# Row sums moved behind the eighth up product, and layer 1's key and value products split into a pass for the latents and a pass for the context

## The chip, the cores and the metric

The kernel runs on one core of one Trainium2 chip. The metric is device time in microseconds (us), the median of the runs. A core has a matmul engine (PE; its weight loads are shown as PEld), a vector engine (DVE), a scalar engine (ACT), GpSimd (POOL) and a sync engine (SP) on whose queue all the loads of this kernel are issued. Each engine works through its own instructions in a fixed order; semaphores tie the engines together.

## The reference

Two layers of a diffusion transformer run over 256 latent tokens and 256 context tokens (512 columns here, latents first), with a model width of 1024. What matters is this part of each layer:

```
mod = silu(c) @ W_mod + b_mod                  # six vectors of 1024, for latents (c) and for context (c_ctx)
h   = rms_norm(x) * (1 + mod_scale) + mod_shift
k, v of four token mixers come from h @ W_in   # first used here: keys and values of the neighbourhood mixer
... attention, gates, output projection, x = x + mod_gate * y
h   = rms_norm(x) * (1 + mod_scale2) + mod_shift2
u   = h @ W_up                                 # 2 x 2816 columns: 22 pairs of 128-column tiles g, v
u   = depthwise conv of 3 taps along the tokens
x   = x + mod_gate2 * ((silu(g) * v) @ W_down)
```

`W_mod` gives 48 tiles of 128 outputs per layer. In layer 1 the context is needed for keys and values only.

## The kernel before, in words

Every matrix product is made of three matmuls per 128-row slice: high parts times high parts, and the two mixed terms with a low part (`mm3`, lines L278, L279, L280). So the weights are split on arrival: `wload` loads a raw tile of 128x1024 (L264, SP's queue), ACT casts its high part `wh` (L272) and DVE subtracts to give the low part `wl` (L257). There are four buffers each for raw, high and low weight tiles. The accumulators `acc` have three buffers of 512 columns in PSUM, `av` one.

The normed activations are made chunk by chunk, eight chunks of 128 channels, by `modulate`: DVE makes `t`, ACT makes the high part `hh` (L423), DVE makes the low part `hl`. The factor of the norm comes by `rstd`: PE sums over the partitions into `tp` (L402), DVE makes `v` (L404), POOL makes `r`, PE spreads it into `sc` (L408), from which DVE reads it for each `t`. That is done for the latents and for the context apart.

`mods` makes modulation vectors by row sums: it loads a 128x1024 tile of `W_mod` (L339, SP's queue, its own pool of four buffers in the stretch that matters here) and DVE multiplies it by the conditioning vector and sums along the row (L349, output `junk`, in the trace one long instruction and the short read of its accumulator). Inside layer 0's FFN there are 56 tiles with 80 row sums: 24 tiles with two sums each, 32 tiles with one. They are the gate of layer 0's FFN and vectors of layer 1.

The FFN of layer 0 begins with four up tiles whose weights are held while they run over the latents' 256 columns and then over the context's 256 columns: eight products of 24 matmuls of 256 columns. Then 40 up products of 512 columns follow (24 matmuls each), the first eight products of the down projection after the first 20 up tiles, and the rest of it at the end. The first three half-width products run together, chunk by chunk, as the modulated chunks come in. After each up product `conv` evacuates it: ACT makes `u`, and DVE adds two taps (`u<-acc`, L254). The product's `acc` is free after the second tap. In the code the eight half-width products come first, then the other products are written interleaved with `mods`. A scheduler moves instructions within each engine against that order, and in the kernel before it put many row sums ahead: 32 of the 80 ran during the output projection and the eight half-width products.

Layer 1 begins with `nakv`, the keys and values of the first mixer: four token tiles (0 and 1 latents, 2 and 3 context) over eight chunks, four accumulators open at once, all four advanced chunk by chunk. The products `naq` (256 wide) follow.

Of the kernel before, what the change touches and what calls it, by code (L numbers as in the profile page):

```python
# [3 lines left out]

# [9 lines left out]
ALU = mybir.AluOpType  # L14
# [5 lines left out]
P = 128  # L20
KD = D // P
# [210 lines left out]
def backbone(ctx: ExitStack, tc, wb, xT, cc, cb, sm, rg, bias, cst, out):  # L232
# [15 lines left out]
    V, A, G = nc.vector, nc.scalar, nc.gpsimd  # L248

    def spool(es, name, bufs, **k):  # L250
        return es.enter_context(tc.tile_pool(name=name, bufs=bufs, reuse_waits="tile", **k))

    def stt(out, in0, scalar, in1, op0, op1):
        V.scalar_tensor_tensor(out=out, in0=in0, scalar=scalar, in1=in1, op0=op0, op1=op1)  # L254

    def tt(e, out, a, b, op):
        e.tensor_tensor(out=out, in0=a, in1=b, op=op)  # L257

    def lo_of(lo, full, hi):
        tt(V, lo, full, hi.bitcast(F32), ALU.subtract)  # L260

    def wraw_load(l, key, n=1024):
        r = wraw.tile([P, 1024], F32, name="raw")
        nc.sync.dma_start(out=r[:, :n], in_=wb[l, KIDX[key], :, :n])  # L264
        return r

    def wload(l, key, k, n):

        w = k * n
        r = wraw_load(l, key, w)  # L270
        h = whi.tile([P, 1024], F32R, name="wh")
        A.copy(h[:, :w], r[:, :w])  # L272
        lo = wlo.tile([P, 1024], F32R, name="wl")
        lo_of(lo[:, :w], r[:, :w], h[:, :w])
        return tuple(z[:, :w].rearrange("p (k n) -> p k n", k=k) for z in (h, lo))

    def mm3(ps, a, b, first, last):
        mm(ps, lhsT=a[0], rhs=b[0], start=first, stop=False)  # L278
        mm(ps, lhsT=a[0], rhs=b[1], start=False, stop=False)  # L279
        mm(ps, lhsT=a[1], rhs=b[0], start=False, stop=last)  # L280

    def drive(*gens):

        live = [[g, n, 0] for g, n in gens]
        while live:
            e = min(live, key=lambda e: (e[2] + 0.5) / e[1])
            try:
                next(e[0])
                e[2] += 1
            except StopIteration:  # L290
                live.remove(e)
# [17 lines left out]
    cact = const.tile([P, 2, D], F32, name="cact")  # L309
    junk = const.tile([P, D], mybir.dt.bfloat16, name="junk")  # L310
    hh = hp.tile([P, KD, T], F32R, name="hh")
    hl = hp.tile([P, KD, T], F32R, name="hl")
# [3 lines left out]
    def small(l):  # L316
        smts[l] = lay.tile([P, NSM], F32, name="smt")
        nc.sync.dma_start(out=smts[l], in_=sm[l])
        Ms[l] = lay.tile([P, 48, 2], F32, name="M")
# [6 lines left out]
    plan = [(l, m, c) for l, m in [(0, 2), (0, 4), (0, 3), (0, 5), (1, 1), (1, 0), (1, 2), (1, 4), (1, 3), (1, 5)]  # L326
            for c in range(KD)]

    def mods(n, raws, ahead=0):


        todo = [plan.pop(0) for _ in range(n)]
        got = []

        def load():
            l, m, c = todo[len(got)]
            r = raws.tile([P, 1024], F32, name="raw")
            g = [g for g in range(3) if m in MOD_GROUPS[g]][0]
            nc.sync.dma_start(out=r, in_=wb[l, KIDX["mod", g, c, MOD_GROUPS[g].index(m)]])  # L339
            got.append(r)  # L340

        for i, (l, m, c) in enumerate(todo):
            while len(got) < min(i + 1 + ahead, n):
                load()
            r, M = got[i], Ms[l]
            ns = 1 if l == L - 1 and m > 1 else 2
            for st_ in range(ns):
                o = M[:, 8 * m + c, st_:st_ + 1]
                V.scalar_tensor_tensor(out=junk, in0=r, scalar=1.0, in1=cact[:, st_], op0=ALU.mult,  # L349
                                       op1=ALU.mult, accum_out=o)  # L350
            if c == KD - 1:
                b0 = SM["bmod"][0] + 8 * m
                bm = smts[l][:, b0:b0 + 8].unsqueeze(2).to_broadcast([P, 8, ns])
                tt(V, M[:, 8 * m:8 * m + 8, :ns], M[:, 8 * m:8 * m + 8, :ns], bm, ALU.add)
            yield

    def some(gen, n):

        for _ in range(n):
            next(gen)  # L360
            yield
# [34 lines left out]
    def rstd(accs, part):  # L396

        a, b, _ = part
        nt = (b - a) // P
        tp = tp_p.tile([P, T], F32, name="tp")  # L400
        for t in range(nt):
            mm(tp[:, t:t + 1], lhsT=accs[a][:, t * P:(t + 1) * P], rhs=ones[:, 0:1], start=True, stop=True)  # L402
        v = tiny.tile([P, 16], F32, name="v")
        V.tensor_scalar(out=v[:, :nt], in0=tp[:, :nt], scalar1=1.0 / D, scalar2=EPS, op0=ALU.mult, op1=ALU.add)  # L404
        r = pow_mhalf(v[:, :nt], nt)
        bc = sc_p.tile([P, T], F32, name="sc")
        for t in range(nt):
            mm(bc[:, t * P:(t + 1) * P], lhsT=r[:, t:t + 1].to_broadcast([P, P]), rhs=ident, start=True, stop=True)  # L408
        return bc
# [7 lines left out]
    def modulate(xt, bc, s1, M, msh, c, part):  # L417

        a, b_, s = part
        hs = tmp.tile([P, T], F32, name="t")[:, :b_ - a]  # L420
        b = M[:, 8 * msh + c, s:s + 1]
        stt(hs, xt[:, c, a:b_], s1[:, c, s:s + 1], bc[:, :b_ - a], ALU.mult, ALU.mult)
        A.activation(out=hh[:, c, a:b_], in_=hs, func=AF.Identity, bias=b)  # L423
        stt(hl[:, c, a:b_], hs, b, hh[:, c, a:b_].bitcast(F32), ALU.add, ALU.subtract)
# [55 lines left out]
    FULL = [(0, 256, 0), (256, 512, 1)]  # L480
    for l in range(L):
# [6 lines left out]
        if l == 0:  # L488
# [4 lines left out]
            xt = x0p.tile([P, KD, T], F32, name="x0")  # L493
# [12 lines left out]
        smt, M = smts[l], Ms[l]  # L506
        vec = lambda n, j=0, p=P: smt[:p, SM[n][0] + j:SM[n][0] + j + 1]
        gam1 = smt[:, SM["n1"][0]:SM["n1"][0] + 8]
        s1 = lay.tile([P, 8, 2], F32, name="s1")
        if l:  # L510
            mod_scale(M, gam1, 1, s1)
        else:
            mods_chunk(0)
            bcs = [rstd(accs, p_) for p_ in FULL]
# [401 lines left out]
        A2 = [0, 1]  # L916

        kv = [(acc_p if t < 3 else av_p).tile([P, 512], F32, name="acc" if t < 3 else "av") for t in range(4)]
        w = None
        for c in range(KD):  # L920
            if l == 0:
                if c:
                    mods_chunk(c)
                V.tensor_scalar(out=s1[:, c], in0=M[:, 8 + c], scalar1=1.0, scalar2=gam1[:, c:c + 1],
                                op0=ALU.add, op1=ALU.mult)
            for bc, p_ in zip(bcs, FULL):
                modulate(xt, bc, s1, M, 0, c, p_)
            if c % 2 == 0:
                w = wload(l, ("nakv", c // 2), 2, 512)
            for t in range(4):  # L930
                mm3(kv[t], tuple(z[:, c, t * P:(t + 1) * P] for z in (hh, hl)), tuple(z[:, c % 2] for z in w),
                    c == 0, c == KD - 1)

        rt = lay.tile([P, 2, 2, 2, RW], F32, name="rt", bufs=1)
        rgt = tmp.tile([P, 4, RW], F32, name="t")
# [18 lines left out]
        for t in range(4):  # L954
            p3 = kv[t].rearrange("p (a n) -> p a n", a=1)
            use_v("na")(t, 1, p3[:, :, 256:])
            later.extend([f, 0] for f in use_nk(t, 1, p3[:, :, :256]))
        first = chain(win_block(l, "naq", qh, use_qk(qT, "na", 4, 64, *q64, None, e=V)), flush())
        drive((first, 1))
        early = lambda n: [(mods(n, wraw), n)] if l == 0 else []  # L960
        newV("df"); newkq("df")
        PAIR = [(0, 1), (2, 3)]
# [26 lines left out]
        if l == 0:  # L989
            xp = ctx.enter_context(tc.tile_pool(name="xt", bufs=1, reuse_waits="tile"))  # L990
            xt = xp.tile([P, KD, T], F32, name="xt")
# [56 lines left out]
        s1 = lay.tile([P, 8, 2], F32, name="s1")  # L1048
# [7 lines left out]
        acts = {}  # L1056

        us = {}

        def up_ps(ff, w_, a, b):  # L1060
            ps = acc_p.tile([P, T], F32, name="acc")
            for kt in range(KD):
                mm3(ps[:, a:b], tuple(z[:, kt] for z in w_), (hh[:, kt, a:b], hl[:, kt, a:b]), kt == 0, kt == KD - 1)
            return ps

        def conv(ff, ps, a, b):

            cw = smt[:, SM["conv"][0] + 4 * ff:SM["conv"][0] + 4 * ff + 4]
            if ff not in us:
                us[ff] = up_.tile([P, T], F32, name="u%d" % (ff // NF))  # L1070
            u = us[ff]
            A.activation(out=u[:, a:b], in_=ps[:, a:b], func=AF.Identity, scale=cw[:, 1:2], bias=cw[:, 3:4])
            u3 = u[:, a:b].rearrange("p (s t) -> p s t", t=256)
            p3 = ps[:, a:b].rearrange("p (s t) -> p s t", t=256)
            stt(u3[:, :, 1:256], p3[:, :, 0:255], cw[:, 0:1], u3[:, :, 1:256], ALU.mult, ALU.add)
            stt(u3[:, :, 0:255], p3[:, :, 1:256], cw[:, 2:3], u3[:, :, 0:255], ALU.mult, ALU.add)

        def up_act(f):
            g, v = us.pop(f), us.pop(NF + f)
# [57 lines left out]
        if not last:  # L1137
            small(l + 1)
            accs = {}
            body = ffn(accs)  # L1140
            drive((some(body, 8), 8))
            mrp = spool(fes, "mr", 4)
            drive((body, 70), (mods(56, mrp, 2), 59))
        else:
            drive((ffn(None), 68))
        fes.close()
        if not last:
            bcs = accs["bc"]
# [22 lines left out]
```

## Time and profile before

| | |
|---|---|
| median of 3 runs | 1481.22 us (1481.22 to 1482.71) |
| profiled execution | 1481.19 us |
| its span, first to last instruction | 1479.4 us |
| PE busy | 1428.8 us, 97% of the span |
| DVE, ACT, POOL busy | 71%, 45%, 14% |
| mean granted clock of PE | 0.989 of full speed |

The shares are means over the whole span. In the stretches at the start of layer 0's FFN (about 565 to 609 us) and at the start of layer 1 (947 to 978 us) PE has gaps, and there it also ran at less than full clock.

### The profile page before, as it was taken

The numbers are of one execution on the slowest core, as the hardware profiler recorded it, in microseconds if no ns is written. First come the engines' busy times: TensorE is split into PE (matmuls) and PEld (weight loads), VectorE is DVE, ScalarE is ACT, GpSimd is POOL, SyncE is SP. The second block draws the span as 40 slices with busy tenths as digits, with TensorE's granted clock in tenths as the row PEclk, the third lists the DMA queues.
The fourth block names the chain that finished last, engine by engine and source line by source line (L and its number), as shares of the span: only waits on it lengthen the run. The fifth ranks groups of instructions, "written<-read, shape, count | busy, mean of one in ns | idle before, by whom it ended". The sixth has DMA issues, their size and how long they took to land.

```text
span 1479.4 us, 22328 instructions
## 1 busy us (share of the span) xinstructions
PE 1428.8 (97%) x8526; PEld 1197.5 (81%) x8526; DVE 1054.5 (71%) x1911; ACT 667.5 (45%) x1197; POOL 204.3 (14%) x191
## 2 busy tenths in 40 slices
PE   6999999999999997999999999899999999899999
PEld 3787777776777887888888888798788889799999
DVE  5688676658776589999856553668777575787884
ACT  5445544444333333444134432356646544564662
POOL 0343001213111200000000000034122331000000
PEclk9999999999999998999999999999999999999999
DMA  9532122214234364568822322333232344455553
GB/s 377 189 103 77 45 88 68 83 53 133 86 114 165 135 218 152 193 221 272 282 94 92 99 93 79 107 101 121 72 104 93 115 140 132 132 182 184 180 179 113
DMA packets 57931, 202.19 MB, mean 137 GB/s; under 512 B 6561, under 2 KB 8097, under 8 KB 57185
## 3 DMA queue, kind: packets, MB, share of 16 engines
q1 hardware_dynamic: 57824, 200.77, 40.2%
q8 instruction: 67, 1.10, 0.3%
q14 instruction: 40, 0.32, 0.1%
HBM read 199.69 MB, written 1.05 MB: 136 GB/s over the span
## 4 chain that ended last, share of the span: by engine, by line
PE 88%; DVE 6%; issue 3%; ACT 2%; DMA 1%; POOL 0%; SPq 0%; POOLq 0%; DVEq 0%; ACTq 0%
PE acc L278 24%; PE acc L280 24%; PE acc L279 24%; PE av L834 3%; PE sc L753 3%; PE tp L826 2%; DVE junk L349 2%; PE sc L768 2%; PE sc L767 1%; DVE wl L257 1%; ACT wh L272 1%; DVE t L254 1%; DMA raw<-in_wb_dram 1%; DMA mraw<-in_wb_dram 1%; PE acc L729 1%
## 5 line engine op out<-in xcount | busy, mean ns | idle before, releaser
L272 ACT CAST wh<-raw 128x1024 fp32r<-128x1024 f32 (+1 forms) x272 | 279.8, 1029 | 438.2 <-PE acc L279 336.6
L257 DVE TENSOR_TENSOR wl<-raw,wh 128x1024 fp32r<-128x1024 f32 (+1 forms) x272 | 331.4, 1218 | 158.7 <-ACT wh L272 156.3
L278 PE MATMUL acc<-hh,wh 128*128 128x256 f32 (+1 forms) x1248 | 424.7, 342 | 15.8 <-DVE u L254 8.7
L279 PE MATMUL acc<-hl,wh 128*128 128x256 f32 (+1 forms) x1248 | 419.4, 337 | 0.8 <-DVE hl L254 0.8
L280 PE MATMUL acc<-hh,wl 128*128 128x256 f32 (+1 forms) x1248 | 420.1, 337 | 0.0
L278 PEld LDWEIGHTS acc<-hh,wh 128*128 128x128 f32 x1248 | 239.8, 193 | 44.5 <-issue 12.9
L279 PEld LDWEIGHTS acc<-hl,wh 128*128 128x128 f32 x1248 | 240.6, 193 | 26.6 <-issue 3.3
L280 PEld LDWEIGHTS acc<-hh,wl 128*128 128x128 f32 x1248 | 240.5, 193 | 26.5 <-issue 4.3
L257 POOL TENSOR_TENSOR r<-v,mhalf 128x4 f32<-128x4 f32 (+3 forms) x59 | 81.6, 1387 | 736.5 <-DVE v L404 461.8
L349 DVE SCALAR_TENSOR_TENSOR junk<-raw,cact 128x1024 bf16<-128x1024 f32 x128 | 156.8, 1225 | 21.7 <-DMA raw<-in_wb_dram 21.1
L278 PE MATMUL acc<-wh,hh 128*128 128x256 f32 (+3 forms) x496 | 148.8, 300 | 4.2 <-ACT hh L423 4.2
L279 PE MATMUL acc<-wl,hh 128*128 128x256 f32 (+3 forms) x496 | 147.5, 297 | 0.0
L280 PE MATMUL acc<-wh,hl 128*128 128x256 f32 (+3 forms) x496 | 145.1, 298 | 0.1
L279 PE MATMUL acc<-al,wh 128*128 128x256 f32 (+1 forms) x370 | 121.5, 328 | 0.0
L278 PE MATMUL acc<-ah,wh 128*128 128x256 f32 (+1 forms) x370 | 121.5, 328 | 0.0
L280 PE MATMUL acc<-ah,wl 128*128 128x256 f32 (+1 forms) x370 | 121.4, 328 | 0.0
L254 DVE SCALAR_TENSOR_TENSOR u<-acc,smt,u 128x255 f32<-128x255 f32 (+1 forms) x184 | 108.4, 593 | 1.5
L278 PEld LDWEIGHTS acc<-wh,hh 128*128 128x128 f32 x496 | 94.9, 191 | 14.1 <-ACT hh L423 7.1
L776 ACT ACTIVATE p<-sc,nm 128x512 f32<-128x512 f32 (+1 forms) x120 | 74.1, 618 | 66.0 <-DVE nm L773 37.9
L280 PEld LDWEIGHTS acc<-wh,hl 128*128 128x128 f32 x496 | 94.5, 191 | 9.4 <-issue 5.5
L279 PEld LDWEIGHTS acc<-wl,hh 128*128 128x128 f32 x496 | 95.0, 191 | 6.8 <-issue 4.6
L773 DVE TENSOR_REDUCE nm<-sc 128x1 f32<-128x512 f32 (+1 forms) x120 | 71.1, 597 | 35.4 <-PE sc L768 24.8
(165 smaller groups left out, 2067.7 us busy)
## 6 DMA issues: line engine op xcount, KB each, us to landing
raw<-in_wb_dram SPq DMA_DIRECT2D x328, 512.0 KB, 3.4
mraw<-in_wb_dram SPq DMA_DIRECT2D x16, 512.0 KB, 10.2
raw<-in_wb_dram SPq DMA_DIRECT2D x20, 384.0 KB, 2.9
x<-in_xT_dram SPq DMA_DIRECT2D x2, 1024.0 KB, 6.3
bt<-in_bias_dram SPq DMA_DIRECT2D x8, 256.0 KB, 3.2
xt<-in_xT_dram SPq DMA_DIRECT2D x2, 1024.0 KB, 7.1
raw<-in_wb_dram SPq DMA_DIRECT2D x4, 320.0 KB, 2.8
cact<-in_cb_dram SPq DMA_DIRECT2D x1, 1024.0 KB, 11.4
```

Of the source, the lines that this page charges most:

```text
L254: V.scalar_tensor_tensor(out=out, in0=in0, scalar=scalar, in1=in1, op0=op0, op1=op1)
L257: e.tensor_tensor(out=out, in0=a, in1=b, op=op)
L272: A.copy(h[:, :w], r[:, :w])
L278: mm(ps, lhsT=a[0], rhs=b[0], start=first, stop=False)
L279: mm(ps, lhsT=a[0], rhs=b[1], start=False, stop=False)
L280: mm(ps, lhsT=a[1], rhs=b[0], start=False, stop=last)
L349: V.scalar_tensor_tensor(out=junk, in0=r, scalar=1.0, in1=cact[:, st_], op0=ALU.mult, op1=ALU.mult, accum_out=o)
L753: mm(sps[:, :n], lhsT=q[o:o + d, c:c + P], rhs=k[o:o + d, T - n:], start=True, stop=True)
L768: mm(sps[:, :n], lhsT=q[r1, 4 + i, c:c + P], rhs=kk[r1], start=False, stop=True)
L773: V.tensor_reduce(out=nm, in_=sps[:, :n], op=ALU.max, axis=AX.X, negate=True)
L776: A.activation(out=p[:, :n], in_=sps[:, :n], func=AF.Exp, bias=nm, accum_out=s)
L834: mm(av[64 * j:64 * j + 64], lhsT=V_[:, 4 - nk + i, vcol(hd):vcol(hd) + 64], rhs=PTs[j][:, i], start=i == 0, stop=i == nk - 1, tile_positi ...
```

## The change

The first part: the second tap of each `conv` is remembered in a list `behind`, and the `mods` call inside the FFN gets the last one that the eight half-width products left, the second tap of the eighth. Every row sum of the 56 tiles is given an ordering edge behind it. The loads of those tiles are given no such edge.

The second part: in layer 1 only, `nakv` first modulates the latents and makes the products of token tiles 0 and 1 for all eight chunks, keeping the four weight tiles; then it modulates the context and makes the products of tiles 2 and 3 for all eight chunks.

```
-    def mods(n, raws, ahead=0):
+    def mods(n, raws, ahead=0, behind=None):
...
-                V.scalar_tensor_tensor(out=junk, in0=r, scalar=1.0, in1=cact[:, st_], op0=ALU.mult,
-                                       op1=ALU.mult, accum_out=o)
+                with tc.issue_after(behind) if behind is not None else nullcontext():
+                    V.scalar_tensor_tensor(out=junk, in0=r, scalar=1.0, in1=cact[:, st_], op0=ALU.mult,
+                                           op1=ALU.mult, accum_out=o)
...
-        w = None
+        w = []
+
+        def kv_mm(c, t):
+            mm3(kv[t], tuple(z[:, c, t * P:(t + 1) * P] for z in (hh, hl)), tuple(z[:, c % 2] for z in w[c // 2]),
+                c == 0, c == KD - 1)
...
             for bc, p_ in zip(bcs, FULL):
-                modulate(xt, bc, s1, M, 0, c, p_)
+                if l == 0 or p_[2] == 0:
+                    modulate(xt, bc, s1, M, 0, c, p_)
             if c % 2 == 0:
-                w = wload(l, ("nakv", c // 2), 2, 512)
-            for t in range(4):
-                mm3(kv[t], tuple(z[:, c, t * P:(t + 1) * P] for z in (hh, hl)), tuple(z[:, c % 2] for z in w),
-                    c == 0, c == KD - 1)
+                w.append(wload(l, ("nakv", c // 2), 2, 512))
+            for t in range(4) if l == 0 else range(2):
+                kv_mm(c, t)
+        if l:
+            for c in range(KD):
+                modulate(xt, bcs[1], s1, M, 0, c, FULL[1])
+                for t in range(2, 4):
+                    kv_mm(c, t)
...
-            stt(u3[:, :, 0:255], p3[:, :, 1:256], cw[:, 2:3], u3[:, :, 0:255], ALU.mult, ALU.add)
+            tap = stt(u3[:, :, 0:255], p3[:, :, 1:256], cw[:, 2:3], u3[:, :, 0:255], ALU.mult, ALU.add)
+            behind.append(tap.ins)
...
-            drive((body, 70), (mods(56, mrp, 2), 59))
+            with_order = mods(56, mrp, 2, behind[-1])
+            drive((body, 70), (with_order, 59))
```

The numbers of instructions on every engine stay the same. The orders change as follows (lines of the changed kernel are one higher from L349 on).

On DVE, at the start of layer 0's FFN, the kernel before has this (a number at the end is a count of like instructions in a row):

```order
668 L349 SCALAR_TENSOR_TENSOR junk,M<-raw,cact 128x1024
669 L257 TENSOR_TENSOR wl<-raw,wh 128x1024
670 L254 SCALAR_TENSOR_TENSOR t<-xt,s_5389,sc 128x256 x2
671 L257 TENSOR_TENSOR ss<-ss,t 128x256
672 L349 SCALAR_TENSOR_TENSOR junk,M<-raw,cact 128x1024
673 L254 SCALAR_TENSOR_TENSOR hl<-t,M,hh 128x256
674 L254 SCALAR_TENSOR_TENSOR t<-xt,s_5389,sc 128x256
675 L254 SCALAR_TENSOR_TENSOR hl<-t,M,hh 128x256
676 L349 SCALAR_TENSOR_TENSOR junk,M<-raw,cact 128x1024
```

At the same place the changed kernel has this:

```order
652 L257 TENSOR_TENSOR wl<-raw,wh 128x1024
653 L254 SCALAR_TENSOR_TENSOR t<-xt,s_5389,sc 128x256 x2
654 L257 TENSOR_TENSOR ss<-ss,t 128x256
655 L254 SCALAR_TENSOR_TENSOR hl<-t,M,hh 128x256
656 L254 SCALAR_TENSOR_TENSOR t<-xt,s_5389,sc 128x256
657 L254 SCALAR_TENSOR_TENSOR hl<-t,M,hh 128x256
```

The row sums between the modulates are gone from here; the order of the rest is nearly the same.

On DVE, where the eighth half-width product (`u_5601`) has been evacuated, the changed kernel begins with the row sums, and from there on carries two of them, seldom one or three, in each of the next 38 products:

```order
696 L257 TENSOR_TENSOR wl<-raw,wh 128x1024
697 L254 SCALAR_TENSOR_TENSOR u_5601<-acc,smt,u_5601 128x255 x2
698 L350 SCALAR_TENSOR_TENSOR junk,M<-raw,cact 128x1024
699 L257 TENSOR_TENSOR u_5572<-u_5572,u_5601 128x512
700 L350 SCALAR_TENSOR_TENSOR junk,M<-raw,cact 128x1024
701 L257 TENSOR_TENSOR wl<-raw,wh 128x1024
702 L350 SCALAR_TENSOR_TENSOR junk,M<-raw,cact 128x1024
703 L257 TENSOR_TENSOR al<-u_5572,ah 128x512
704 L254 SCALAR_TENSOR_TENSOR u_5763<-acc,smt,u_5763 128x2x255
705 L350 SCALAR_TENSOR_TENSOR junk,M<-raw,cact 128x1024
```

So all 80 sums stand here and behind, where the kernel before had 48. On SP's queue the first four tiles of `W_mod` are issued where they were; behind them the changed kernel has twelve weight tiles in a row, and only then the fifth tile of `W_mod`, after which the two kinds alternate.

On PE, at the start of layer 1, the kernel before has the latents' `sc` products first, then the context's `tp`, and the context's `sc` after the first two products of chunk 0:

```order
4071 L408 MATMUL sc<-C,r 128x128 x2
4072 L402 MATMUL tp<-C,ss 128x1 x2
4073 L278 MATMUL acc<-wh,hh 128x512
4074 L279 MATMUL acc<-wl,hh 128x512
4075 L278 MATMUL acc<-wh,hh 128x512
4076 L279 MATMUL acc<-wl,hh 128x512
4077 L280 MATMUL acc<-wh,hl 128x512 x2
4078 L408 MATMUL sc<-C,r 128x128 x2
```

The changed kernel has the context's `tp` inside chunk 0, goes on with the latents' chunks 1, 2 and 3 from row 4079 on, and has the context's `sc` only in chunk 3, at row 4093:

```order
4072 L409 MATMUL sc<-C,r 128x128 x2
4073 L278 MATMUL acc<-wh,hh 128x512
4074 L279 MATMUL acc<-wl,hh 128x512
4075 L278 MATMUL acc<-wh,hh 128x512
4076 L279 MATMUL acc<-wl,hh 128x512
4077 L403 MATMUL tp<-C,ss 128x1 x2
4078 L280 MATMUL acc<-wh,hl 128x512 x2
4079 L278 MATMUL acc<-wh,hh 128x512
```

Nothing on PE stands between the latents' `sc` and their first product any more. DVE's order there begins as before with a `wl` and then has two latents' `t`, the context's last `ss`, and latents' `hl` and `t` in turn.

## Rows read from the trace of the kernel before

**Rows 1.** Waits of PE, 560 to 660: us in total, times, longest

```profile
PE acc L278 <- DVE u L254: 8.7, 2, 5.9
```

**Rows 2.** PE's timeline, start of layer 0's FFN: start, duration, instruction, [idle before]

```profile
565.08 0.60 PE L408 MATMUL sc<-C,r 128*128 128x128 f32 x4
569.56 0.62 PE L278 MATMUL acc<-hh,wh 128*128 128x256 f32 x3 [3.88 <-ACT hh L423]
...
588.91 0.55 PE L278 MATMUL acc<-hh,wh 128*128 128x256 f32 x1 [5.94 <-DVE u L254]
...
605.79 0.36 PE L278 MATMUL acc<-hh,wh 128*128 128x256 f32 x1 [2.71 <-DVE u L254]
...
608.94 0.47 PE L278 MATMUL acc<-hh,wh 128*128 128x512 f32 x1
```

**Rows 3.** Busy time by stretch, start of layer 0's FFN

```profile
core 0: us, PE busy (x) PEld busy (x) DVE busy (x) ACT busy (x) POOL busy (x), PEclk, DMA share, GB/s
...
569.50:577.20 7.70, 6.87 (x34) 6.79 (x35) 7.70 (x18) 2.34 (x6) 0.69 (x1) 0.57 0.51 151
...
588.90:594.40 5.50, 5.49 (x26) 5.50 (x27) 5.50 (x13) 1.52 (x3) 0.00 (x0) 0.50 0.28 86
...
605.80:608.94 3.14, 3.09 (x25) 2.92 (x25) 3.14 (x7) 1.97 (x3) 0.00 (x0) 1.00 0.98 360
```

**Rows 4.** DVE's timeline, start of layer 0's FFN

```profile
567.36 1.22 DVE L257 TENSOR_TENSOR wl<-raw,wh 128x1024 fp32r<-128x1024 f32 x1
568.49 0.87 DVE L254 SCALAR_TENSOR_TENSOR t<-xt,s,sc 128x256 f32<-128x256 f32 x2
...
569.61 1.22 DVE L349 SCALAR_TENSOR_TENSOR junk<-raw,cact 128x1024 bf16<-128x1024 f32 x1
...
570.76 0.48 DVE L254 SCALAR_TENSOR_TENSOR hl<-t,M,hh 128x256 fp32r<-128x256 f32 x1
...
588.29 1.25 DVE L254 SCALAR_TENSOR_TENSOR u<-acc,smt,u 128x255 f32<-128x255 f32 x3
```

**Rows 5.** ACT's timeline, the weight cast ahead of it

```profile
565.16 1.04 ACT L272 CAST wh<-raw 128x1024 fp32r<-128x1024 f32 x1 [1.44 <-PE acc L279]
```

**Rows 6.** Line L349 alone: stretch, us, DVE busy (count), PEclk, DMA share, GB/s

```profile
524.00:607.10 83.10, 39.10 (x64) 0.92 0.57 191
607.10:740.00 132.90, 58.81 (x96) 1.00 0.75 249
```

**Rows 7.** Busy time by stretch, full-width products (columns as in Rows 3)

```profile
607.10:740.00 132.90, 132.85 (x593) 110.14 (x593) 124.86 (x203) 48.02 (x62) 0.00 (x0) 1.00 0.75 249
...
660.00:680.00 20.00, 20.00 (x89) 16.54 (x89) 19.99 (x33) 7.52 (x11) 0.00 (x0) 1.00 0.84 274
```

**Rows 8.** Waits of SP's queue, 600 to 760

```profile
SPq L339 <- DVE junk L349: 69.2, 37, 4.4
```

**Rows 9.** PE's timeline, start of layer 1

```profile
951.40 0.60 PE L402 MATMUL tp<-C,ss 128*128 128x1 f32 x4 [3.31 <-DVE ss L257]
...
955.93 0.79 PE L278 MATMUL acc<-wh,hh 128*128 128x512 f32 x1 [1.11 <-ACT hh L423]
...
978.22 0.28 PE L278 MATMUL acc<-wh,hh 128*128 128x256 f32 x1
```

**Rows 10.** DVE's timeline, start of layer 1

```profile
949.79 0.48 DVE L254 SCALAR_TENSOR_TENSOR t<-xt,s,sc 128x256 f32<-128x256 f32 x1
```

**Rows 11.** Busy time by stretch, start of layer 1 (columns as in Rows 3)

```profile
955.93:959.50 3.57, 3.57 (x8) 2.81 (x9) 3.57 (x10) 2.16 (x5) 0.00 (x0) 0.50 0.00 0
```

**Rows 12.** PE's timeline, layer 1's FFN, two more gaps

```profile
1276.39 0.58 PE L402 MATMUL tp<-C,ss 128*128 128x1 f32 x4 [2.71 <-DVE ss L257]
...
1292.81 0.36 PE L278 MATMUL acc<-hh,wh 128*128 128x256 f32 x1 [2.01 <-ACT u L1072]
```

**Rows 13.** Busy time by stretch, behind those two gaps (columns as in Rows 3)

```profile
1277.20:1283.90 6.70, 4.78 (x20) 4.48 (x21) 4.63 (x12) 2.72 (x6) 0.71 (x1) 0.50 0.19 70
...
1294.10:1297.60 3.50, 3.50 (x19) 3.50 (x18) 1.60 (x5) 1.38 (x3) 0.00 (x0) 0.51 0.81 265
```

More of the change, by code (lines that the diff above doesn't have):

```diff
@@ L1 @@
-from contextlib import ExitStack
+from contextlib import ExitStack, nullcontext
 import math
@@ L253, in stt @@
     def stt(out, in0, scalar, in1, op0, op1):
-        V.scalar_tensor_tensor(out=out, in0=in0, scalar=scalar, in1=in1, op0=op0, op1=op1)
+        return V.scalar_tensor_tensor(out=out, in0=in0, scalar=scalar, in1=in1, op0=op0, op1=op1)
     def tt(e, out, a, b, op):
@@ L1058, in backbone @@
         us = {}
+        behind = []
         def up_ps(ff, w_, a, b):
```

## The prediction, written before the changed kernel was run

> **What bounds the kernel now.** PE is busy for 97% of the span, so the first view to read is the waits of PE: time can be won where PE stands still, or where it runs at half clock. Around the first part of the change the waits of PE [rows 1] name DVE's `u`, 8.7 us in two waits. The timeline of PE [rows 2] puts them in place: after the last `sc` product (565.08 + 0.60 = 565.7) PE is idle for 3.9 us until `hh` comes, then 5.9 us before the fourth half-width product, 2.7 us before the eighth, and the first full-width product starts at 608.94. So 43.3 us lie between 565.7 and 608.94, for eight products of 24 matmuls at 0.12 us (25 in 3.09 us [rows 3]), 23.0 us of work at full clock. The view by stretches [rows 3] gives the rest: at 569.5 and 588.9 the clock is 0.57 and 0.50 (1.2 GHz of 2.4), and DVE is busy without a pause. DVE is the bound here. Its timeline [rows 4] shows with what: row sums of 1.15 us (569.61 to 570.76, less what overlaps) between the `t` and `hl` of the modulates and between the taps `u`. In 524 to 607 the row sums take 39.1 us [rows 6], counted in pairs of rows: 32 sums.
>
> In the second place PE's timeline [rows 9] shows a gap of 3.3 us before the context's `tp`, one of 1.1 us before the context's `hh`, and a slow stretch [rows 11]; the next products, `naq`, start at 978.22.
>
> **The first part, step by step.** *The first gap.* The last weight cast ends at 565.16 + 1.04 = 566.2 [rows 5]. In the new order its `wl` follows with no row sum before it, 566.2 to 567.35 (it took 567.36 to 568.49 [rows 4]), then come two `t`. Before, the first `hh` matmul (569.56 [rows 2]) started 1.07 us after the first `t` started (568.49); that gives 568.4, a gap of 2.7 us, and 1.1 us won.
>
> *The first three products.* `t`, `t`, `ss`, `hl` take 0.79 + 0.33 + 0.39 us (568.49 to 569.61 is two `t` and `ss`; 0.39 from one third of the three `u` at 588.29, 1.25 us [rows 4], whose shape is nearly that of `hl`). So the first `hl` is there at 568.9. From then on a chunk costs DVE 0.79 us and PE 9 matmuls, 1.1 us: DVE runs ahead, and PE is the bound. 72 matmuls of 0.12 with the `tp` between (0.5) end near 577.9.
>
> *The second gap.* The fourth product needs the first one's `acc`: ACT's `u` (0.5, a third of its three), then by DVE's order five operations of 0.39 (tap, tap of the second product, `t`, `hl`, tap), 2.0 us. It starts near 580.3, with a gap of 2.4 us where there were 5.9.
>
> *The rest.* Five products of 2.9 us follow, in each of which DVE has two taps and some modulates (0.8 + 1.6 us) and no row sum: no wait, the third gap of 2.7 us is gone. The first full-width product would start at 580.3 + 14.4 = 594.7. That is 14.2 us before 608.94, if the clock is full.
>
> *The clock.* Both remaining gaps are near the size of those where rows differ: after 2.7 us at 605.79 the clock stayed at 1.00 [rows 2, 3], after 2.7 at 1276.39 and 2.0 at 1292.81 [rows 12] PE ran at 1.2 GHz, busy for 4.8 and 3.5 us [rows 13], of which half is lost: 0, 2.4, 1.75, a mean of 1.4 us for a gap. The bounds are nothing and what the slow stretches of before cost: 6.87 x 0.43 = 2.95 and 5.49 x 0.5 = 2.75 [rows 3]. I take 2 x 1.4, because the gaps have the size of the three. The first part is worth 14.2 - 2.8 = 11.4, bounds 8.5 and 14.2.
>
> The Trainium skill, on the page "TensorE: Matmul & The Clock Gate" (section "HAM oscillation — how this bites in real kernels"), speaks against counting on a full clock: a wait between two bursts of matmuls can throttle the array, so that the next burst starts cold, and half of the throttled time is lost. By that rule every gap left here costs a slow stretch, and the total below would be 10.1 instead of 14.6. The trace agrees in all these gaps except the one at 605.79.
>
> *What the moved row sums cost.* All 80 now stand in 38 products in a row, of which the first follows the eighth half-width one (two per product, in the order); a product takes 24 matmuls of 0.224 us (593 in 132.85 [rows 7]), 5.4 us, so 38 take 204 us. In 607 to 740 DVE was busy 124.86 of 132.9 us [rows 7], 58.81 of them with 48 sums [rows 6], 1.225 each. So other work took 0.50 of the time; 80 sums in 204 us add 0.48. DVE would be 0.98 busy. That is close, but below one, and in 660 to 680 DVE was 19.99 of 20 busy with PE never idle [rows 7]; three `acc` buffers and four weight tiles give PE a store of two products. SP's queue now issues two tiles of `W_mod` and one of weights per product, 1.57 MB in 5.4 us, 290 GB/s; it moved 274 in 660 to 680 [rows 7]. The loads L339 waited for row sums 37 times, 69.2 us [rows 8], with weights queued behind them, and PE did not wait. I take nothing for it. The cover is those stores: if they run out, each product is longer by DVE's excess.
>
> **The second part.** Before, `tp` of the context stood ahead of the first product and waited for `ss`. Now the first `hh` matmul comes 1.07 us after `t` at 949.79 [rows 10], at 950.9. The context's `tp` and `sc` lie in PE's order where their inputs are ready: its modulates have until the end of the latents' pass, 48 matmuls or 10.8 us. 96 matmuls of 0.225 and `tp`, `sc` (1.1) end at 973.6; `naq` started at 978.22: 4.6 won. The span from 951.40 to 978.22 is 26.8 us, of which 21.6 + 1.1 are work and 1.1 a gap, so 3.0 was clock. One gap of about 2.9 us stays before the first product: 1.4 as above, bounds 0 and 3.0. The second part is worth 3.2, bounds 1.6 and 4.6.
>
> **The sum.** 11.4 + 3.2 = 14.6 us, from the profiled execution's 1481.19 (the median is 1481.22): 1466.6.
>
> **The rivals.**
> *No slow clock behind the shorter gaps.* The gap at 605.79 speaks for it, the two in layer 1 against. 14.2 + 4.6 = 18.8: 1462.4.
> *Every gap left is followed by a slow stretch as before.* 8.5 + 1.6 = 10.1: 1471.1. For it speak five of the six gaps over 2 us [rows 2, 9, 12], against it the one at 605.79. The Trainium skill's rule on the clock gate, named above, ends here.
> *DVE becomes the bound of the full-width products.* It is 0.98 busy by the sum above, and the new loads are asked for later (twelve weight tiles stand before the fifth tile of `W_mod`). If each sum waited 0.3 us for its tile, DVE would need 0.98 x 5.4 + 2.1 x 0.3 = 5.9 us per product, 0.5 over, and 38 products would take 20 us more: 1466.6 + 20 = 1487, slower than before. It decides from 14.6 / 38 = 0.4 us per product. Against it stands 607 to 740, where the same queue, at 0.36 sums per us against 0.39, cost PE nothing.
> *The order does not help in one part.* If the scheduler's order on DVE or ACT made the context's chunks late, the second part would give nothing: 1469.8. If the second gap stayed 5.9 us, because `u` waits on ACT behind queued `hh`, the first would give 3.5 less: 1470.1.
>
> **How the numbers follow.** Chances: the forecast with its mixture of clocks 0.5, full clock 0.12, slow everywhere 0.17, one part without effect 0.11, DVE as the bound 0.10, of which half ends above 1481. Two hundredths of the rest of that case lie within 0.2% of no change, about 3 us, which is what a measurement of this kernel can tell. So faster 0.93, same 0.02, slower 0.05. The range leaves out the tail of the bound DVE and the last of full clock: 1461.5 to 1473.5.
>
> **What would show it.** In the waits of PE: `u` near 2.4 us in one wait instead of 8.7 in two, and `hh` below 3; the first full-width product 10 to 14 us earlier after the last `sc`. By stretches: PE full with DVE at 0.95 and more in the following 200 us. At the start of layer 1: no wait for `ss`, and `naq` 2 to 5 us sooner after the latents' `sc`. It is wrong if waits of PE for `u` or `wl` appear in the 38 products behind the eighth, if `junk` waits for loads there, or if the clock falls in places where it was full before.

## The result, and the profile after

The changed kernel takes 1467.15 us (median of 4 runs, 1466.79 to 1468.31) against 1481.97 us (median of 4, 1481.22 to 1483.61): a ratio of 0.9902, 95% interval 0.9890 to 0.9915, 14.8 us faster. The forecast was 1466.6 us, 14.6 us faster. The profiled execution takes 1467.0 us, its span is 1465.2. Line numbers from L349 on are higher by one, further down by more.

**Start of layer 0's FFN.** The waits of PE between 560 and 660 in the changed kernel (us in total, times, longest) answer to [rows 1]:

```profile
PE acc L278 <- ACT hh L424: 2.8, 1, 2.8
PE acc L278 <- DVE u L254: 2.4, 1, 2.4
```

One wait for `u` is left of the two, and it is 2.4 us long. PE's timeline of the same kernel gives the places, against [rows 2] (rows left out are marked):

```profile
566.34 0.60 PE L409 MATMUL sc<-C,r 128*128 128x128 f32 x4
...
569.82 0.62 PE L278 MATMUL acc<-hh,wh 128*128 128x256 f32 x3 [2.77 <-ACT hh L424]
...
582.00 0.36 PE L278 MATMUL acc<-hh,wh 128*128 128x256 f32 x1 [2.42 <-DVE u L254]
...
597.96 0.40 PE L278 MATMUL acc<-hh,wh 128*128 128x512 f32 x1
```

From the end of the last `sc` (566.94) to the first full-width product are 31.0 us, where there were 43.3: 12.2 us won. Busy time by stretch (columns as in [rows 3]) shows how much half clock was in them:

```profile
570.00:578.00 8.00, 8.00 (x69) 8.00 (x70) 8.00 (x22) 4.55 (x11) 0.69 (x1) 1.00 0.17 63
...
582.00:586.00 4.00, 4.00 (x21) 4.00 (x22) 2.60 (x7) 0.51 (x1) 0.00 (x0) 0.57 0.00 0
```

After the first gap PE ran at full clock, after the second at 0.57 for some 4 us. The rule of the Trainium skill that the prediction weighed ("TensorE: Matmul & The Clock Gate", section "HAM oscillation — how this bites in real kernels": a wait between bursts can make the next one start cold), applied to every gap as the prediction's rival did, would have made both slow; the trace agrees for one of the two. The waits in that section's own example, 3 to 5 us, are longer than both gaps.

**The moved row sums.** The first two rows are line L350 alone (stretch, us, DVE busy and count, clock, DMA share, GB/s), the other two are stretches with all engines, from the first full-width product to layer 1:

```profile
524.00:598.00 74.00, 0.00 (x0) 0.98 0.33 112
598.00:820.00 222.00, 98.09 (x160) 1.00 0.67 224
...
597.96:820.00 222.04, 222.04 (x982) 183.92 (x981) 212.49 (x332) 83.27 (x107) 0.00 (x0) 1.00 0.67 224
820.00:936.40 116.40, 116.40 (x568) 98.69 (x567) 60.45 (x93) 38.93 (x55) 0.70 (x1) 1.00 0.27 91
```

All 80 sums (160 rows, with the accumulator reads) run in 598 to 820, DVE is busy for 212.5 of 222.0 us, and PE has not one gap up to layer 1. From the first full-width product to the end of layer 1's first `sc` it takes 339.1 us in both kernels (948.09 - 608.94 = 339.15 before, 937.02 - 597.96 = 339.06 now).

**Start of layer 1.** In the kernel before, the latents' `sc` ended at 948.09:

```profile
947.49 0.60 PE L408 MATMUL sc<-C,r 128*128 128x128 f32 x4
```

PE's timeline in the changed kernel, against that row and [rows 9], and a stretch (columns as in [rows 3]):

```profile
936.42 0.60 PE L409 MATMUL sc<-C,r 128*128 128x128 f32 x4
...
939.79 0.50 PE L278 MATMUL acc<-wh,hh 128*128 128x512 f32 x1 [2.76 <-ACT hh L424]
...
964.24 0.28 PE L278 MATMUL acc<-wh,hh 128*128 128x256 f32 x1
```

```profile
941.00:945.00 4.00, 4.00 (x13) 3.29 (x14) 4.00 (x12) 2.52 (x6) 0.88 (x1) 0.59 0.13 53
```

One gap of 2.8 us is left, with half clock behind it. From the end of `sc` to the first `naq` matmul are 27.2 us, where there were 30.1 (948.09 to 978.22): 2.9 us won. But further on, in the attention of layer 1, waits of PE appear that the kernel before did not have. Here are all that the changed kernel has in 1005 to 1090:

```profile
PE av L835 <- DVE PT L587: 0.8, 1, 0.8
PE sc L768 <- ACT p L777: 0.6, 1, 0.6
PE tp L878 <- ACT st L875: 0.5, 1, 0.5
```

The kernel before has one row in the stretch that answers to it (1015 to 1105):

```profile
PE sc L768 <- DVE qS L257: 0.2, 1, 0.2
```

How much longer the attention takes shows in the distance from `naq` to the first `tp` of layer 1's FFN. In the kernel before it is 298.2 us (978.22 to 1276.39 [rows 9, 12]), in the changed kernel 299.8 (964.24 to 1263.99):

```profile
1263.99 0.58 PE L403 MATMUL tp<-C,ss 128*128 128x1 f32 x4 [2.71 <-DVE ss L257]
```

**The sum of the two profiles.** 12.2 (FFN) + 0.1 (up to layer 1) + 2.9 (start of layer 1) + 0.2 (all behind, 501.2 to 501.0) - 1.3 (up to the last `sc` before the FFN: 565.7 to 566.9) = 14.2 us of span, 1479.4 to 1465.2. The 1.3 comes for the most part from a stretch near 58 us, where the change touches nothing, with a clock of 0.58 over 3.4 us (57.4 to 60.8); the kernel before ran at full clock there.

### The profile page after: what moved, and what is told of

Its sections match the earlier page's. It is cut to its first block, busy times and chain, and to the rows that moved or that the text cites. A ratio compares the mean times of both kernels' runs of the same rounds, so it can differ in the third digit from the quotient of the medians.

```text
span 1465.2 us, 22330 instructions
## 1 busy us (share of the span) xinstructions
PE 1424.0 (97%) x8526; PEld 1193.7 (81%) x8526; DVE 1053.9 (72%) x1911; ACT 665.6 (45%) x1197; POOL 203.8 (14%) x191
## 4 chain that ended last, share of the span: by engine, by line
PE 93%; issue 2%; DVE 2%; ACT 2%; DMA 1%; POOL 0%; SPq 0%; POOLq 0%; DVEq 0%; ACTq 0%
PE acc L278 26%; PE acc L280 26%; PE acc L279 25%; PE av L835 3%; PE sc L754 3%; PE tp L827 2%; PE sc L769 2%; PE sc L768 2%; DVE wl L257 1%; PE acc L730 1%; DMA mraw<-in_wb_dram 1%; ACT wh L272 1%; PE acc L690 1%; PE tp L372 0%; PE tp L608 0%
## 5 line engine op out<-in xcount | busy, mean ns | idle before, releaser
L279 PEld LDWEIGHTS acc<-hl,wh 128*128 128x128 f32 x1248 | 238.4, 191 | 25.6 <-issue 3.3
L350 DVE SCALAR_TENSOR_TENSOR junk<-raw,cact 128x1024 bf16<-128x1024 f32 x128 | 157.1, 1227 | 17.0 <-DMA raw<-in_wb_dram 16.4
L278 PEld LDWEIGHTS acc<-wh,hh 128*128 128x128 f32 x496 | 95.2, 192 | 15.1 <-ACT hh L424 8.3
## 6 DMA issues: line engine op xcount, KB each, us to landing
cact<-in_cb_dram SPq DMA_DIRECT2D x1, 1024.0 KB, 11.4
```

## The experiments

All times are medians with the ratio to the kernel before on the same chip and its 95% interval; stretches are from the one profile of each. The runs were made in groups on three chips, so versions of different groups are compared by their ratios.

**The sums alone.** The second part is undone (the loop over chunks and four tiles of the kernel before).

> The changed kernel with its second part undone: the row sums stand behind the eighth up product, layer 1's key and value products run all four token tiles chunk by chunk as before. Theory (the two parts are separate, the second is worth 2.9 us of the changed kernel's gain): 1467.15 + 2.9 = 1470.0, ratio to before 0.992; at the start of layer 1 PE waits 3.3 us for the context's ss and 1.1 us for its hh again. Rival (the second part does nothing, what looked like its gain was the clock): 1467.2, within 1 us, with naQ's first matmul again as early behind the latents' sc.

1468.2 us, ratio 0.9907 (0.9890 to 0.9924). From the last `sc` to the first full-width product of layer 0's FFN are 31.0 us, as in the changed kernel, so the first part alone gives that gain. At the start of layer 1 the two old gaps are back, 3.24 us and 1.11 us; the first in PE's timeline:

```profile
940.08 0.61 PE L403 MATMUL tp<-C,ss 128*128 128x1 f32 x4 [3.24 <-DVE ss L257]
```

`naq` comes 29.0 us after `sc`, 1.8 later than in the changed kernel. But its waits of PE in 1005 to 1090 are this one row:

```profile
PE sc L769 <- DVE qS L257: 0.2, 1, 0.2
```

In the changed kernel 1.9 us of new waits stand there. All that is behind the start of `naq` takes 498.95 us here and 500.96 in the changed kernel; up to the first `tp` of layer 1's FFN it is 298.2 us, as in the kernel before, against 299.8. So neither theory was right: the second part does win at its place, and gives about as much back, most of it within 130 us.

**The passes alone.**

```
-            with_order = mods(56, mrp, 2, behind[-1])
+            with_order = mods(56, mrp, 2)
```

> The changed kernel with its first part undone: the row sums have no edge, layer 1 has the two passes. Theory: only the second part's 2.9 us are won, 1482.0 - 2.9 = 1479.1, ratio 0.998; the three gaps of 3.9, 5.9 and 2.7 us at the start of layer 0's FFN are back. Rival (the first part's gain comes from a shift of the scheduler's order that any edit would have given): below 1474.

1482.97 us, ratio 1.0009 (0.9993 to 1.0024): no gain, where 2.9 us were expected. The waits of PE at the start of layer 0's FFN are nearly those of the kernel before, and the stretch to the first full-width product takes 43.4 us:

```profile
PE acc L278 <- DVE u L254: 8.9, 2, 6.2
PE acc L278 <- ACT hh L424: 3.9, 1, 3.9
PE acc L279 <- DVE hl L254: 1.4, 3, 0.8
```

Together with the sums alone (31.0 us) that shows where the first part's gain comes from. The start of layer 1 takes 25.6 us in place of 30.1, at full clock, so 4.5 us are won at that place. But in 1015 to 1105 PE waits again, for 2.4 us:

```profile
PE av L835 <- DVE PT L587: 1.2, 2, 0.7
PE sc L768 <- ACT qS L583: 0.8, 1, 0.8
PE sc L768 <- ACT p L777: 0.4, 1, 0.4
```

From `naq` to the first `tp` of layer 1's FFN are 300.6 us, 2.4 more than in the kernel before.

**More sums.** The tiles that have one sum get it twice, 112 in place of 80.

```
-            for st_ in range(ns):
+            for st_ in [0, 0] if behind is not None and ns == 1 else range(ns):
```

> The changed kernel with 32 more row sums: each W_mod tile that has one sum gets it twice (the same result is written again), 112 sums in place of 80, 39 us more of DVE. The scheduler strings them out over 18 more products, still two per up product. Theory (a density of two sums per product of 5.4 us is what DVE can carry beside its other work): PE keeps without a wait in the FFN, time 1467.2 within 1.5 us. Rival (DVE at 0.98 is at its limit and the changed kernel only just gets by): waits of PE for u or wl appear, and up to 39 - 4 = 35 us are lost, 1475 to 1502.

1467.99 us, ratio 0.9905 (0.9889 to 0.9921). The theory held; busy time by stretch:

```profile
600.84:820.00 219.16, 219.16 (x969) 181.49 (x968) 212.18 (x332) 81.91 (x105) 0.00 (x0) 1.00 0.61 197
820.00:939.00 119.00, 119.00 (x578) 100.76 (x578) 95.24 (x157) 39.33 (x58) 0.70 (x1) 1.00 0.45 145
```

DVE is busy for 95.2 us of the second stretch, where it was 60.5, and PE has no gap in either. The scheduler still gives about two sums per product, and more sums only last longer.

**Sums forced.** Each first tap of the full-width products is ordered behind the last sum written before it, and `mods` is driven twice as fast.

```
...
+                summed.append(one.ins)
...
+            with tc.issue_after(summed[-1]) if l == 0 and b - a == T else nullcontext():
+                stt(u3[:, :, 1:256], p3[:, :, 0:255], cw[:, 0:1], u3[:, :, 1:256], ALU.mult, ALU.add)
...
-            drive((body, 70), (with_order, 59))
+            drive((body, 70), (with_order, 118))
...
```

> The changed kernel with the row sums forced: mods is driven twice as fast, and in the 512-wide up products the first tap on DVE is ordered behind the last row sum written before it, so that the first 16 full-width products carry about three sums each; nothing is left out. By the order DVE has 6.7 to 7.0 us of work in each of these 16 products, PE 5.4. Theory (above one, DVE sets the pace, at the excess less a store of one or two products): 16 x 1.4 = 22, less 5 to 8, so 14 to 22 us slower than the changed kernel, 1481 to 1489, with PE waiting for u. Rival (the stores of acc and weights take it up, DVE's load does not matter): 1467 to 1470.

1486.01 us, ratio 1.0033 (1.0019 to 1.0046): slower than the kernel before, in the expected range. Waits of PE in 590 to 960, and busy time by stretch:

```profile
PE acc L278 <- DVE u L254: 9.7, 4, 3.4
PE acc L278 <- DVE s L257: 1.8, 1, 1.8
PE acc L278 <- ACT u L1087: 1.6, 1, 1.6
```

```profile
600.65:700.00 99.35, 87.86 (x370) 70.92 (x369) 97.01 (x153) 35.66 (x47) 0.00 (x0) 0.97 0.59 196
```

The stretch from the first full-width product to layer 1 takes 357.0 us in place of 339.1. 13.1 of the 17.9 us are the waits shown, and part of the rest is half clock behind them (0.97 over the first 99 us). So the same 80 sums can make DVE the bound: they cost this when about three of them stand in a product and the taps have to stand behind them. The run changes the density and the order together and does not tell which of the two costs how much.

**Behind the fourth product.** `behind[3]` in place of `behind[-1]`.

> The changed kernel with the row sums behind the fourth up product in place of the eighth. By the order one sum then stands in each of the products 5 to 8 and two ahead of them; DVE has 3.1 to 3.4 us of work in each, PE 2.9. Theory (what matters is that no sum lies between the modulates and the first taps; one sum per half-width product nearly fits): at most 1 us slower or equal, 1466 to 1468.5. Rival (each sum in front of the eighth product delays PE by its 1.2 us): 4 to 6 sums, 5 to 7 us slower, 1472 to 1474, with PE waiting for u before the fifth to eighth product.

1468.1 us, ratio 0.9909 (0.9894 to 0.9923). The waits of PE in 560 to 660 are the changed kernel's, to the tenth: 2.8 us for `hh` and 2.4 for `u`, each in one wait. Line L350 is busy for 4.9 us between 583 and 600, so four sums and the start of a fifth ran ahead of the first full-width product and no wait came of them. The sums need not wait for the eighth product; with the passes alone beside it, this says that what matters is that they stay out of the modulates and the first taps. From `sc` to the first full-width product are 33.8 us here, not 31.0, with the same two gaps: there was half clock behind both, which also gave DVE more time beside these products. That value, 33.7 to 33.9, also came in three other runs with the same gaps (more sums, sums forced, and the context lagging, below).

**The fourth product in `av`.** The first of four tries at the gaps that are left. `spare` is true for the fourth of the latents' up products alone.

```
...
-            ps = acc_p.tile([P, T], F32, name="acc")
+            ps = av_p.tile([P, T], F32, name="av") if spare else acc_p.tile([P, T], F32, name="acc")
...
```

> The changed kernel with the fourth latents' up product accumulated in the buffer av, which is unused there, so that it need not wait for the first product's acc; PE runs four products chunk by chunk. Theory (the gap of 2.42 us is the wait for the acc, and the half clock behind it, 1.7 us, goes with it): 2.4 to 4.1 us faster than the changed kernel, 1463.0 to 1464.7. Rival (the wait moves on to the fifth product, which then needs the first acc after the same DVE work): within 1 us of 1467.2, with a gap of about 2 us one product later.

1469.11 us, ratio 0.9915 (0.9900 to 0.9930), no gain. The gap of 2.42 us is gone, and this one stands before the eighth product:

```profile
593.19 0.36 PE L278 MATMUL acc<-hh,wh 128*128 128x256 f32 x1 [1.53 <-ACT u L1084]
```

The stretch becomes 30.1 in place of 31.0 us; in layer 1 it has the longer set of new waits (2.7 us). The theory fell. The rival had it right that the wait moves on, but it came before the eighth product and not the fifth, and the time is above the rival's range.

**The fourth `wl` later.** It is ordered behind the first `hl`, which `lows[0]` names.

```
...
-                ws = [up_w(ff) for ff in lst]
+                ws = [up_w(ff) for ff in lst[:3]]
+                with tc.issue_after(lows[0]):
+                    ws.append(up_w(lst[3]))
...
```

> The changed kernel with the low part wl of the fourth up weight ordered on DVE behind the first hl, in place of ahead of the first t. Theory (the first gap is the chain xt, wl, t, hh; 1.14 us of it is this wl): the gap of 2.77 us becomes 1.6, the kernel 1.1 us faster, 1466.0; if PE ran at half clock behind it, nothing changes in that. Rival (wl is needed by then, or DVE is late afterwards and the wait comes back at hl): within 0.3 us of 1467.2.

1467.11 us, ratio 0.9902 (0.9885 to 0.9918). In PE's timeline the first gap shrinks as expected, and `hl` takes a part back:

```profile
568.16 0.62 PE L278 MATMUL acc<-hh,wh 128*128 128x256 f32 x3 [1.51 <-ACT hh L424]
...
570.66 0.39 PE L279 MATMUL acc<-hl,wh 128*128 128x256 f32 x1 [0.37 <-DVE hl L254]
```

The stretch is 30.6 us, 0.4 less. In the time it does not show, which is the rival's case.

**All three** (the two above, and in layer 1 the fourth key and value weight's `wl` behind the first `hl`).

> The changed kernel with the fourth latents' product in av, the fourth up weight's wl behind the first hl, and in layer 1 the fourth key and value weight's wl behind the first hl as well. Theory (the three gaps are apart and add up): 2.4 to 4.1, 1.1 and 1.1 us, so 4.6 to 6.3 us faster than the changed kernel, 1460.9 to 1462.6, ratio to before 0.986 to 0.987. Rival (shorter waits are replaced by the next): more than 1464.

1465.26 us, ratio 0.9888 (0.9874 to 0.9903), less than the theory gave and in the rival's range. The FFN's stretch is 28.6 us and the start of layer 1 24.6, both at full clock; but the gaps are not gone. The FFN has 1.51 us before the first product, 0.51 before the fifth, and this before the eighth:

```profile
592.31 0.36 PE L278 MATMUL acc<-hh,wh 128*128 128x256 f32 x1 [1.89 <-ACT u L1088]
```

and what lies behind `naq` takes 503.5 us, 2.5 more than in the changed kernel.

**The changed kernel again, and three on the same chip.**

> The changed kernel once more, beside the next three on the same chip. Expected as before: 1467.2 within 1.5 us, ratio 0.990; at the start of layer 1 the second part wins 1.8 us against the sums alone, and 0.8, 0.65 and 0.5 us of new waits of PE between 1005 and 1090 (for DVE's PT, ACT's p and st) give 1.8 to 2.0 back.

1465.72 us, ratio 0.9898 (0.9880 to 0.9915). The new waits are the same. With the same program the half clock fell elsewhere:

```profile
570.00:578.00 8.00, 8.00 (x57) 8.00 (x56) 8.00 (x22) 4.32 (x9) 0.70 (x1) 0.79 0.04 15
...
582.00:586.00 4.00, 3.75 (x31) 3.78 (x32) 2.85 (x8) 1.13 (x3) 0.00 (x0) 1.00 0.00 0
```

Behind the first gap it was slow, behind the second at full clock, the other way round than in the first profile, with the same 31.1 us in all.

> The sums behind the eighth up product, the fourth latents' product in av and the fourth up weight's wl behind the first hl, but layer 1 chunk by chunk as before the change. Theory (the second part is worth nothing in the end, because its order brings new waits later): the span behind the naQ products is 499 us in place of 501 to 503.5, the start of layer 1 is 29 in place of 24.6 to 27.2, so the whole is within 1.5 us of the version with all three (1465.3). Rival (the second part's 3 us stay won): 2.5 to 4 us slower than it, 1468 to 1469.

1468.41 us, ratio 0.9907 (0.9893 to 0.9922), 3.2 us above the version with all three, which was run on another chip; by the ratios it is 2.8 us, and the intervals overlap. That is the number of the rival. Its profile speaks for the mechanism of the theory all the same: in 1005 to 1090 PE waits 0.2 us, and from `naq` to the first `tp` of layer 1's FFN are 298.2 us, both as with the sums alone. What made it slow is the start of layer 1, 31.4 us, with a clock of 0.80 over 942.3 to 952, and with the old order it also lacks the edit of layer 1's `wl` (a gap of 2.8 us in the changed kernel, 1.35 in the version with all three). From the first `sc` of layer 1's FFN to the end it took 201.3 us against 198.4, though the two do not differ in code there. The run does not separate these.

> The changed kernel with the context following the latents by three chunks in layer 1, in place of a pass of its own behind all eight. PE's order is that of the changed kernel up to chunk 3, and all four accumulators end close together as in the kernel before. Theory (the early end of the latents' keys and values is what reorders the mixers behind and brings the waits of 2.0 us): the start of layer 1 stays 25.6 to 27.2 us, and the waits between 1005 and 1090 go back to 0.2: 2 us faster than the changed kernel, 1465.3. Rival (the scheduler's order behind changes with any edit, and waits of 1 to 2 us come with it): within 1 us of the changed kernel, with other waits there.

1469.29 us, ratio 0.9915 (0.9900 to 0.9930). Neither number came, and the effect that the theory asked for did not: the waits in 1005 to 1090 are back in the same three places:

```profile
PE sc L768 <- ACT p L777: 0.7, 1, 0.7
PE av L835 <- DVE PT L587: 0.5, 1, 0.5
PE tp L878 <- ACT st L875: 0.5, 1, 0.5
```

But the edit does less than was expected of it. In PE's timeline the latents' accumulators end about 4.5 us ahead of the context's, which is nearer than in the changed kernel (10.9 us) and not as close as in the kernel before (about 1.4 us). So it weakens the theory and does not settle it. A wait of 0.65 us for the context's `hh` came on top, and half clock behind both gaps of layer 0's FFN (33.7 us).

> The version with all three edits and the context following by three chunks. Theory: what the two give adds up, 2 us below the version with all three: 1463.3, ratio 0.9875. Rival (other waits come in layer 1): 1465 or more.

1464.54 us, ratio 0.9881 (0.9866 to 0.9896), between the theory's number and the rival's. The waits in the attention are there (2.4 us), as the rival had it. It is the lowest ratio, but its interval overlaps with those of the changed kernel (0.9890 to 0.9915 and 0.9880 to 0.9915): no version was shown to be faster.

## Why the prediction was right

**The gaps of the FFN.** The chain worked out from the order and the durations of before held to a tenth: 2.77 us for the first gap (2.7 forecast), 2.42 for the second (2.4), none for the third. DVE's five operations before the fourth product ran as listed, from 579.74 to 581.77, 2.0 us. One sum in between was off: 568.4 + 72 x 0.12 + 0.5 is 577.5 and not 577.9, and it leaves out the context's `sc` (0.6 us), which also lies there. From the first `hh` product to the second gap are 9.8 us, where 9.5 were forecast. With the sums left where they were, all three gaps are there (the passes alone).

**The clock.** By the forecast the stretch would have been 14.2 us shorter at full clock; it was 12.2, so 2.0 were lost, where the forecast took 2.8 within bounds of 0 and 5.7. The row at 0.57 over 4.0 us accounts for 1.7 of the 2.0. In four other runs with the same gaps the loss was 4.7 to 4.8 (33.8 us), inside the bounds too. The choice of a mean was the right kind of answer, since two profiles of the same program show the half clock in different places.

**The moved sums cost nothing.** 339.15 against 339.06 us. DVE was 0.97 busy over the 204 us forecast for the sums (197.2 us in 598 to 802), not 0.98. The loads of `W_mod` and of weights waited on SP's queue for buffers, and PE waited for no weight. The 290 GB/s of the prediction counts two tiles of `W_mod` per product, but 24 of the 56 tiles carry two sums each: over those 204 us it was 232, and 280 only from 700 on, where tiles with one sum follow. The rival's own condition, each sum waiting 0.3 us for its tile, was not tested. The forced sums cost 17.9 us, near its 20, by another way: three sums in a product, ahead of the taps. So DVE can become the bound here, and that the two numbers are near says no more.

**The second part failed as a net.** At its place it won 2.9 us, near the forecast (3.2), with `hh` again 1.07 us after `t` (938.72 to 939.79). Where no half clock came (the passes alone, more sums, behind the fourth product) the stretch is 25.6 us, 4.5 less than before, where 4.6 were forecast for full clock; the changed kernel's 27.2 have 1.6 us of half clock, where 1.4 were taken. The step that failed is the one that counted only the stretch up to `naq` and let everything behind it start earlier by as much. The order of the mixers behind it changes with it, and in all eleven profiles of kernels in which the latents go ahead of the context PE has 1.7 to 2.7 us of waits for `PT`, `p`, `qS` or `st` in the 85 us that answer to 1005 to 1090, against 0.2 in the three without (before, sums alone, no passes). From `naq` to the first `tp` of layer 1's FFN the three take 298.2 us each, the eleven 299.8 to 302.5. With it alone the ratio is 1.0009 (0.9993 to 1.0024); adding it to the sums takes 0.9907 to 0.9902, inside both intervals. So its 3.2 us in the sum should have been near nothing: by the times no run tells its net from zero.

**Why the sum came out all the same.** In the profile the attention's loss and the 1.3 us of an early half clock are made up in two places. The first part did 0.8 better than forecast (12.2 for 11.4). And layer 1's FFN, which the change does not touch, took 2.4 us less from its first `sc` on: its gap of 2.0 us [rows 12] is 1.5, and of the two slow stretches [rows 13] only the first is there again, as these rows of the changed kernel show (columns as in [rows 3]); the second had cost half of 3.5 us.

```profile
1264.70:1271.50 6.80, 4.78 (x20) 4.49 (x21) 4.70 (x13) 2.72 (x6) 0.71 (x1) 0.53 0.21 72
1280.13:1285.00 4.87, 4.87 (x41) 4.87 (x42) 3.65 (x7) 3.85 (x6) 0.00 (x0) 1.00 0.83 262
```

The medians say the same: the sums alone won 13.4 us (1481.62 to 1468.20, by the interval 11.3 to 16.3), where the first term was 11.4, and the second part added nothing that can be told from noise, where its term was 3.2. So the first part and its mechanism carry the total, the second term was right only at its place, and that 14.8 came within 0.2 us of 14.6 is in part luck.

What stays open: why the scheduler's order of the attention brings these waits. Whether the early end of the latents' keys and values does it was tried in part only (the context lagging): with less than half of that lead the waits stayed. An order of the attention held fixed was not tried.

## What to carry to other kernels

Work with no deadline belongs behind the work that the busiest engine waits for, and an ordering edge behind a named instruction does that. Put it where the engine that does it has room between due instructions: the same sums cost nothing in such gaps and 17.9 us when three stood in a product and the taps behind them. And count a gain won at one place only after reading the waits of the stretches behind it: a reordered loop can return it a hundred microseconds later, where nothing was edited.

## What the runs showed of the hardware

The granted clock after a short gap of PE differs between two profiles of the same program, and so of the same order. Two gaps of 2.77 and 2.42 us were followed by 1.00 and 0.57 in one profile of the changed kernel and by 0.79 (over 570 to 578) and 1.00 in another; in four kernels with the same gaps half clock came after both, and the stretch took 33.8 us instead of 31.0. Here are the rows of the one with more sums, with its gaps at 569.86 and 584.89 (columns as in [rows 3]):

```profile
570.00:578.00 8.00, 8.00 (x45) 8.00 (x46) 6.85 (x19) 3.96 (x9) 0.70 (x1) 0.61 0.17 60
...
586.00:590.00 4.00, 4.00 (x23) 4.00 (x22) 1.74 (x5) 1.07 (x2) 0.00 (x0) 0.57 0.00 0
```

It is not the chip: the sums alone were run on the same chip as more sums, and took 31.0 us. So a difference of 2.8 us between two profiles of such a place can be the clock's alone.
